# Attention in a hybrid decoder block: every second block of 512 queries computed with the keys on the partitions, the others still with weights transposed by DMA

## The chip, the cores and the metric

The kernel runs on one core of one Trainium2 chip. The metric is the device time of one execution in microseconds (us). An engine is named as the profile names it: PE is the matrix engine (its weight loads are PEld), DVE the vector engine, ACT the scalar engine, POOL the general engine and SP the queue engine, which here only issues DMAs.

## What is computed

One layer of a decoder block on 4096 tokens, with 16 learned meta tokens in front. The normalised input is projected; one half of the columns feeds eight attention heads with a forgetting bias, the other eight heads of a recurrence (RWKV-7). Both halves are gated, projected out, added to the input and normalised. The part that the change touches is the attention:

```python
def _fox_block(q, k, v, cq, ck, q_start):
    qb, kb = q.shape[2], k.shape[2]
    s = jnp.einsum('bhqd,bhkd->bhqk', q, k).astype(jnp.float32) / math.sqrt(HEAD_DIM)
    s = s + cq[..., :, None] - ck[..., None, :]
    q_pos = q_start + jnp.arange(qb)
    k_pos = jnp.arange(kb)
    s = jnp.where(k_pos[None, :] <= q_pos[:, None], s, NEG_INF)
    p = jax.nn.softmax(s, axis=-1)
    return jnp.einsum('bhqk,bhkd->bhqd', p, v.astype(jnp.float32))

def fox_branch(p, b_f):
    q, k, v, fl, z = _split(p, FOX_SIZES)
    ...
    log_f = jax.nn.log_sigmoid(fl.astype(jnp.float32) + b_f.astype(jnp.float32))
    c = jnp.cumsum(log_f, axis=1).transpose(0, 2, 1)
    ...
    return (o * jax.nn.silu(z.astype(jnp.float32))).astype(p.dtype)
```

Head dimension 64, 8 heads, causal. The term cq is the same for all keys of a query, so the softmax does not need it; the term ck stays.

## The kernel before

**Stages.** First comes a stage of about 2100 us in which the recurrence runs as a chain of small matmuls, and the input projections run beside it as filler. The projections are cut into four passes over the 17 blocks of the input `u`: pass 0 is what the recurrence needs, pass 1 is q, k, v and gate of head pair 2 (heads 4 and 5), pass 2 is head pairs 0 and 1, pass 3 is head pair 3 and the gate of the recurrence (`gate_block`). A unit is 48 matmuls of 256 columns. Then comes the attention: heads in the order of `HEADS` (4, 5, 0, 1, 2, 3, 6, 7). What is left of passes 2 and 3, and after it `rwkv_out` (32 rows of output projection of the recurrence, 24 matmuls of 512 columns each), is the filler of the first seven heads. Beside the last head and after it stands the output projection of the attention (`out_prep`, `out_rows`), 32 rows again.

**Attention before.** Queries go by tiles of 128 (32 tiles a head, `advance` and `attention`). For a tile with W keys before it (W = 16 + 128(i+1)): PE multiplies the query tile with the keys in pieces of 1024 (two matmuls of 512 columns for each 512 keys, since q is kept as a high and a low half in float16); DVE adds the forgetting bias `cb`, writes the scores `sp` to SBUF and keeps the maximum in `mt` (line 1051, followed by a read of the accumulator); ACT takes the exponential and sums the row (line 1065); ACT copies the high half to float16 (line 1071), POOL (60 in 100) or DVE (40 in 100) makes the low half (line 1076). Now the weights lie with queries on the partitions, and the product with V needs keys there, so SP issues a DMA transpose for each piece of up to 1024 keys, both halves, `ht<-hl` (line 1078). PE then multiplies `ht` with V, for every 128 keys one matmul of 128 columns (high half, V as high and low) and one of 64 (low half). DVE and ACT finish the 64 output columns (lines 1096 to 1101). In the program the product of tile i is written behind the scores of tile i+1.

**Order.** A scheduler puts the instructions of each engine into a fixed order when the kernel is built; `tc.high_priority` sets what goes first (attention 100000, its filler 97000; for the last head attention has 3000). Each engine runs its list strictly in that order and waits where an operand isn't there. Buffers rotate: 6 of `hl`, 6 of `ht`, 9 of `sp`, 2 PSUM tiles of 1024 scores. Loads for attention (Q, K, V, `cb`) are issued on ACT's queue.

Of the kernel before, what the change touches and what calls it, by code (L numbers as in the profile page):

```python
# [37 lines left out]
NREST = 26  # L38
SEG = 1024
CH = 1024  # L40
NHL, NSP = 6, 9
HEADS = (4, 5, 0, 1, 2, 3, 6, 7)
POOL_SHARE = 60
FILL = 1.0
PASS_OF = (2, 2, 1, 3)
# [5 lines left out]
P_SHIFT = 15 * math.log(2.0)  # L51
# [25 lines left out]
def hymba_kernel(ctx: ExitStack, tc, x, meta, norm_w, w_in, b_f, mu_shift, w0, w_up, a0, a_up,  # L77
# [141 lines left out]
    qk_d = [dram.tile([5, P, TP], F16, name=f"qk_d{p}") for p in range(4)]  # L219
# [12 lines left out]
    scs = const.tile([P, 4, 2, 2], F32, name="scs")  # L232

# [5 lines left out]
    with ExitStack() as rs:  # L239
# [223 lines left out]
        def qk_block(p, w, bi, u):  # L463
# [4 lines left out]
            qk = fi.tile([P, 5, NB], F16, tag="qk", name="qk")  # L468
# [3 lines left out]
            for j in range(2):  # L472
                s = w["sq"] if j == 0 else UNSCALE * QK_SCALE
                A.activation(qk[:, 3 * j, :n], ps[:, j, :n], AF.Copy, scale=s)
                V.scalar_tensor_tensor(out=qk[:, 3 * j + 1, :n], in0=ps[:, j, :n], scalar=s, in1=qk[:, 3 * j, :n],
                                       op0=ALU.mult, op1=ALU.subtract)
            G.tensor_copy(qk[:, 2, :n], qk[:, 0, :n])
            fq.dma_start(qk_d[p][:, :, t0:t0 + n].rearrange("a p t -> p a t"), qk[:, :, :n])

        def vz_block(p, w, bi, u):  # L480
# [11 lines left out]
            A.activation(vt[:m, :ns, :, 0, :], pv, AF.Copy, scale=UNSCALE * QK_SCALE)  # L492
            for s in range(ns):
                V.scalar_tensor_tensor(out=vt[:m, s, :, 1, :], in0=pv[:, s], scalar=UNSCALE * QK_SCALE,
                                       in1=vt[:m, s, :, 0, :], op0=ALU.mult, op1=ALU.subtract)
# [53 lines left out]
        def forget():  # L549
# [23 lines left out]
            for j0 in range(0, NJ, 2):  # L573
# [11 lines left out]
                SP.dma_start(c_d[:, j0 * P:(j0 + k) * P], row[:, :k * P])  # L585
                yield 0.1
# [9 lines left out]
            pair_units(0) + pair_units(1),  # L596
            pair_units(3) + [unit(gate_block, wd[4 + j], j) for j in range(2)]]
# [3 lines left out]
                ((2, 2), (1, 0), qk_weights(1, wd[1], wp1)), ((2, 3), (1, 1), vz_weights(1, wd[1], wp1)),  # L601
                ((3, 0), (2, 0), qk_weights(3, wd[3], wp1)), ((3, 1), (2, 1), vz_weights(3, wd[3], wp1)),
                ((3, 2), (2, 2), gate_weights(0, wd[4], wp1)), ((3, 3), (2, 3), gate_weights(1, wd[5], wp1))]
        ended = (-1, 0)
        done = [0] * 4
# [30 lines left out]
        def projections():  # L636
            for i in range(4):
                yield from run_pass(i)
# [323 lines left out]
    with ExitStack() as fs:  # L962
        def apool(name, bufs, **kw):
# [3 lines left out]
        NCH = SEQ // CH  # L967
        fw = apool("fw", 1)
        kv = apool("kv", NCH + 1)
        ps_q = apool("ps_q", 2, space=PSUM)  # L970
# [4 lines left out]
        V.tensor_copy(identb, ident)  # L975
        dmask = fw.tile([P, P], BF16, name="dmask")
        G.memset(dmask, 0.0)
        G.affine_select(out=dmask, in_=dmask, pattern=[[-1, P]], compare_op=ALU.is_ge, fill=-1e30,
                        base=0, channel_multiplier=1)

        def projected(p, t):

            while done[PASS_OF[p]] * NB < min(t, SEQ + 1):
                next(late)

        def head_load(h, c):
# [6 lines left out]
            Kt = kv.tile([P, CH + N_META], F16, tag="K", name="K")  # L993
            for a in range(2):
                DQ.dma_start(Kt[64 * a:64 * a + 64, :n], qk_d[p][3 + a, q0:q0 + 64, ta:ta + n])
# [4 lines left out]
            Vt = kv.tile([P, CH // P + 1, P], F16, tag="V", name="Vt")  # L1000
            DQ.dma_start(Vt[:, :CH // P], v_d[p][ta:ta + CH, hp * P:hp * P + P].rearrange("(j t) e -> t j e", t=P))
            if n > CH:
                DQ.dma_start(Vt[:N_META, CH // P], v_d[p][SEQ:T, hp * P:hp * P + P])
            return Kt, Vt, cb
# [7 lines left out]
        qz = {}  # L1012

        def attention(h, i, head, dst):

            nonlocal nseg
            p, hp = divmod(h, 2)
            q0 = 64 * hp
            if i % 4 == 0:
                g = min(4, NT - i)  # L1020
                t0 = N_META + i * P
# [264 lines left out]
```

## Time and profile before

| | us |
|---|---|
| three runs | 4457.58, 4472.32, 4473.12 |
| median | 4472.32 |
| the profiled execution | 4462.28 |
| its span (first to last instruction) | 4460.4 |
| mean granted PE clock of it | 0.916 |

Busy time in that span: PE 3912.1 us (88%), DVE 2956.9 (66%), POOL 2230.5 (50%), ACT 2122.7 (48%). The difference of about 2 us between the execution's time and its span lies around the first and the last instruction. The first attention score matmul starts at 2122.0 us, the last value product near 4361 us; what follows is output projection alone. "Busy" is the time in which an engine works on at least one instruction; for PE, whose matmuls overlap, it says less than the pace at which matmuls follow each other.

### The profile page before, as it was taken

How to read it: one execution, taken by the hardware profiler on the slowest of the kernel's cores; microseconds unless marked ns; L12 is line 12 of the kernel's file. 1: busy time of each engine (PE TensorE's matmuls, PEld its weight loads, DVE VectorE, ACT ScalarE, POOL GpSimd, SP SyncE). 2: the span in 40 equal slices, each digit the busy share in tenths (PEclk: the TensorE clock that was granted, in tenths of full speed). 3: DMA queues.
4: the chain of work that ended last, by engine and by line, in shares of the span. 5: the costliest groups of instructions: out<-in, count | busy, mean ns of one | idle time of the engine just before them, and what ended most of it. 6: DMA issues, size and time to landing. Idle time of an engine off the chain costs nothing. (4 is left out here: it accounts for less than half of the span.)

```text
span 4460.4 us, 106426 instructions
## 1 busy us (share of the span) xinstructions
PE 3912.1 (88%) x42336; PEld 3012.8 (68%) x42336; DVE 2956.9 (66%) x6217; ACT 2122.7 (48%) x4338; POOL 2230.5 (50%) x3289
## 2 busy tenths in 40 slices
PE   5689999999989899998878878888888878978888
PEld 4577777777767677777656655666666656666566
DVE  5346665666667666752878978677787758646774
ACT  5433333333333233321666757577676747524552
POOL 4137565667666665762445545444454435332340
PEclk8899999999876899899999989999999989989989
DMA  9963223323222344324999999999999999999995
GB/s 265 262 172 93 79 79 97 87 75 90 74 70 79 85 138 121 98 88 141 196 213 229 216 193 227 199 216 227 208 212 234 212 203 223 258 270 242 198 218 185
DMA packets 1702644, 755.37 MB, mean 169 GB/s; under 512 B 1444601, under 2 KB 1639601, under 8 KB 1692162
## 3 DMA queue, kind: packets, MB, share of 16 engines
q1 hardware_dynamic: 1489346, 502.84, 55.8%
q10 hardware_dynamic: 194624, 170.08, 15.3%
q0 software_dynamic: 18176, 75.66, 5.6%
q8 instruction: 332, 5.44, 0.5%
q14 instruction: 166, 1.36, 0.1%
HBM read 278.97 MB, written 158.50 MB: 98 GB/s over the span
## 5 line engine op out<-in xcount | busy, mean ns | idle before, releaser
L1076 POOL TENSOR_TENSOR hl<-sp,hl 128x1024 f16<-128x1024 f32 (+7 forms) x384 | 719.7, 1881 | 517.3 <-ACT hl L1071 440.7
L1065 ACT ACTIVATE sp<-sp,nm 128x1024 f32<-128x1024 f32 (+8 forms) x672 | 644.5, 962 | 223.5 <-DVE nm L1057 175.6
L1071 ACT ACTIVATE hl<-sp 128x1024 f16<-128x1024 f32 (+8 forms) x672 | 568.2, 872 | 366.1 <-DMA ht<-hl 239.4
L92 PE MATMUL ps_o<-Vt,ht 128*128 128x64 f16 (+3 forms) x8960 | 559.5, 211 | 180.6 <-DMA ht<-hl 177.8
L92 PE MATMUL ps_q<-K,Q 128*128 128x512 f16 (+4 forms) x2432 | 596.9, 366 | 119.4 <-DVE mt L1051 118.3
L758 POOL TENSOR_TENSOR tm<-X,Am 128x248 f32<-128x248 f32 (+30 forms) x1023 | 498.1, 487 | 376.6 <-DMA Am<-a_d 290.1
L92 PEld LDWEIGHTS <-ht 128*128 128x128 f16 (+1 forms) x8960 | 466.9, 100 | 315.0 <-DMA ht<-hl 204.9
L92 PEld LDWEIGHTS <-wu 128*128 128x128 f16 (+1 forms) x5476 | 513.1, 102 | 194.8 <-ACT wu L160 28.1
L760 POOL TENSOR_TENSOR X<-X,tm 128x248 f32<-128x248 f32 (+30 forms) x1023 | 517.7, 506 | 76.6
L67 PEld LDWEIGHTS <-wu 128*128 128x128 f16 (+1 forms) x4988 | 454.5, 101 | 114.3 <-issue 26.0
L1051 DVE CUSTOM_DVE_ANT_0 sp<-ps_q,cb,mt 128x1024 f32<-128x1024 f32 (+8 forms) x416 | 436.1, 1048 | 80.3 <-PE ps_q L92 40.8
L1076 DVE TENSOR_TENSOR hl<-sp,hl 128x1024 f16<-128x1024 f32 (+8 forms) x288 | 383.2, 1333 | 99.3 <-ACT hl L1071 98.1
L92 PEld LDWEIGHTS <-Q 128*128 128x128 f16 x2432 | 221.8, 100 | 294.8 <-issue 150.2
L67 PE MATMUL ps_in<-fu,wu 128*128 128x256 f16 x3108 | 416.0, 285 | 3.4 <-DVE car L67 3.4
L1051 DVE CUSTOM_DVE_ANT_0 sp<-ps_q,cb,scs 128x1024 f32<-128x1024 f32 (+7 forms) x256 | 297.6, 1164 | 71.2 <-POOL hl L1076 43.9
L92 PE MATMUL ps_qk<-fu,wu 128*128 128x256 f16 x1632 | 237.7, 280 | 24.0 <-DVE t1k L500 18.5
L92 PE MATMUL ps_vz<-wu,fu 128*128 128x256 f16 x1644 | 247.6, 284 | 1.0 <-ACT th L544 0.6
L92 PE MATMUL ps_p<-OH,yH 128*128 128x512 f32 x512 | 221.5, 433 | 29.0 <-DVE oxt L1144 27.5
L1070 POOL MEMSET hl<- 128x224 f16 x256 | 72.4, 287 | 336.8 <-DMA ht<-hl 318.4
L92 PE MATMUL ps_zr<-fu,wu 128*128 128x256 f16 x1536 | 224.8, 285 | 8.0 <-DVE nm L1057 6.3
L67 PE MATMUL psz<-UV,SC 32*64 32x64 f32 (+1 forms) x4128 | 222.4, 232 | 3.0 <-ACT UV L67 2.2
L92 PE MATMUL ps_p<-OH,yL 128*128 128x512 f32 x512 | 209.6, 411 | 0.0
(350 smaller groups left out, 6976.6 us busy)
## 6 DMA issues: line engine op xcount, KB each, us to landing
fu<-u_d POOLq DMA_DIRECT2D x32, 1024.0 KB, 6.8
fu<-u_d SPq DMA_DIRECT2D x30, 1024.0 KB
pr<-p_d SPq DMA_DIRECT2D x32, 832.0 KB
p_d<-prt SPq DMA_DIRECT2D x96, 256.0 KB
u_d<-u SPq DMA_DIRECT2D x16, 1024.0 KB
Am<-a_d SPq DMA_DIRECT2D x128, 128.0 KB
Q<-qk_d ACTq DMA_DIRECT2D x128, 128.0 KB
oxt<-in_x_dram ACTq DMA_DIRECT2D x32, 512.0 KB
```

The source lines that it names most:

```text
L67: r = f(*args, **kw)
L92: PE.matmul(o, lhsT=l, rhs=r, start=start, stop=stop)
L758: G.tensor_tensor(out=tm[:, :, :k], in0=bc(X[:, :, s:s + 1], [P, 8, k]), in1=bc(Am[:, s * C + s + 1:s * C + C].unsqueeze(1), [P, 8, k]), o ...
L760: G.tensor_tensor(out=X[:, :, s + 1:], in0=X[:, :, s + 1:], in1=tm[:, :, :k], op=ALU.add)
L1051: V.tensor_tensor_reduce(out=sp[:, a - a0:b - a0], in0=ps[:, :b - a], in1=head[c][2][:, a - o:b - o], scale=scs[:, p, 0, hp:hp + 1], scala ...
L1065: A.activation(sp[:, :n], sp[:, :n], AF.Exp, bias=nm[:, 0:1], accum_out=nm[:, 1 + a // SEG:2 + a // SEG])
L1070: G.memset(hl3[:, :, n:], 0.0)
L1071: A.activation(hl3[:, 0, :n], sp[:, :n], AF.Copy)
L1076: eng.tensor_tensor(out=hl3[:, 1, :n], in0=sp[:, :n], in1=hl3[:, 0, :n], op=ALU.subtract)
```

## The change

The eight blocks of 512 queries of a head go by turns. Blocks 1, 3, 5 and 7 (`straight(n)`) are computed as before, in the new function `weights_s`, with these differences: score pieces are 512 wide instead of 1024 (four PSUM tiles of 512 instead of two of 1024), the row sum is no longer made by ACT's accumulator but by a column of ones beside V (products of 129 and 65 columns), and the output is finished once for a block in `finish`. Blocks 0, 2, 4 and 6 are computed in `weights` with the keys on the partitions: PE makes the transposed scores (128 keys by 512 queries) directly, in two matmuls, of which the second also adds the shift by the maximum, carried in rows 64 to 127 of `QL` against a constant in `KB`; ACT's exponential reads PSUM and adds the key's bias from the new tile `cneg` as its per-partition bias; the result already has keys on the partitions and needs no transpose. For the shift the maximum of each query must be known beforehand: `maxima(n+1)`, run beside block n, makes scores once more from the high half alone (one matmul per 512 keys) and reduces them on DVE.

Buffers: `hl` 5, `ht` 4, `sp` 6. The projections now go in five passes, one head pair each (2, 0, 1, 3), with the two gate units beside pairs 0 and 1, so `u` is read once more. `qk_d` loses its third row, and POOL the copy that filled it. A row of `rwkv_out` counts 1.0 instead of 0.5 in the filler's budget, a straight block gets 1.6 times the filler of another, and what `projected` forces ahead is counted. In the last head, rows of output projection are offered after every second step once a block is finished.

```diff
+CH = 1024
+NHL, NSP, NHT = 5, 6, 4
 SEG = 1024
-NHL, NSP = 6, 9
+LAG = 2
+SHARE_S = 1.6
-PASS_OF = (2, 2, 1, 3)
+PASS_OF = (2, 3, 1, 4)
...
-            pair_units(0) + pair_units(1),
-            pair_units(3) + [unit(gate_block, wd[4 + j], j) for j in range(2)]]
+            pair_units(0) + [unit(gate_block, wd[4], 0)],
+            pair_units(1) + [unit(gate_block, wd[5], 1)],
+            pair_units(3)]
...
+    def maxima(n):
...
+            for t in range(NQ):
...
+                    ps = ps_q.tile([P, 512], F32, tag="q", name="ps_m")
+                    mm(ps[:, :e - a], QA[:, t * P:(t + 1) * P], head[c][0][:, a - o:e - o], True, dg == e)
...
+                    V.tensor_tensor_reduce(out=sx[:, :e - a], in0=ps[:, :e - a], in1=head[c][3][:, a - o:e - o],
+                                           scale=1.0, scalar=(-3e38 if ni == 0 else mt[:, ni - 1:ni]),
...
+            psb = ps_q.tile([P, QB], F32, tag="q", name="ps_b")
+            for t in range(NQ):
+                for v in range(2):
+                    mm(psb[64 + 32 * v:96 + 32 * v, t * P:(t + 1) * P], bc(bp[:, t, v:v + 1], [P, 32]), identh)
+            A.activation(QL[64:128], psb[64:128], AF.Copy)
...
+    def weights(n):
...
+            for j0 in range(0, J, 2):
...
+                    ps = ps_q.tile([P, QB], F32, tag="q", name="ps_s")
+                    mm(ps[:k, qa:], head[c][0][:, o:o + k], QA[:, qa:], True, False)
+                    mm(ps[:k, qa:], head[c][1][:, o:o + k], QL[:, qa:], False, r < 0)
...
+                    A.activation(sp[:k, v, qa:], ps[:k, qa:], AF.Exp, bias=cneg[:k, j, h:h + 1],
+                                 scale=scs[:k, p, 0, hp:hp + 1])
...
+                    A.activation(hh[:k, v, qa:], sp[:k, v, qa:], AF.Copy)
+                    nseg += 1
+                    eng = G if nseg * POOL_SHARE % 100 < POOL_SHARE else V
+                    eng.tensor_tensor(out=hl[:k, v, qa:], in0=sp[:k, v, qa:], in1=hh[:k, v, qa:], op=ALU.subtract)
...
+                            mm(po, hh[:kk, v, ts], Vj[:kk, 0:HD2], j == 0 and t % 2 == 0, False)
+                            mm(po[:, HD:], hl[:kk, v, ts], Vj[:kk, HD:HD2], False, t % 2 == 1 and r == t + 1)
...
+                pend.append(out)
+                while len(pend) > LAG:
+                    pend.pop(0)()
...
+    def straight(n):
+        return blocks_a[n][1] % 2 == 1
...
+            u, k = units(n), 0
+            for i, _ in enumerate((weights_s if straight(n) else weights)(n)):
+                while k * u < steps * (i + 1):
+                    next(nxt, None)
+                    k += 1
+                yield
```

Two places in the built order show what moved. The first is DVE's list in the second head of the order, in the block of queries 2576 to 3087 (block 5). Names: `sp` or `spq` are a tile's own scores, `mt` its running maximum, `sx` the scores that only feed a maximum of the block after it; `ISA` with two outputs is the fused add and maximum, `ISA` with one is the read of its accumulator. Before:

```order
L1051 ISA sp_33638,mt_33623<-ps_q_33639,cb_31742,mt_33623,scs_121 128x1024
L1051 ISA mt_33623 128x1
L1096 TENSOR_REDUCE nm_33495<-nm_33495 128x1
L1097 RECIPROCAL nm_33495<-nm_33495 128x1
L1076 TENSOR_TENSOR hl_33413<-sp_33329,hl_33413 128x1024
L503 SCALAR_TENSOR_TENSOR t1k_33293<-t1k_33294,t1k_33293 128x256
L1100 TENSOR_TENSOR o1_33241<-ps_o_33192,o1_33241 128x64
L1076 TENSOR_TENSOR hl_33419<-sp_33337,hl_33419 128x16
L1051 ISA sp_33645,mt_33623<-ps_q_33646,cb_32516,mt_33623,scs_121 128x272
```

And now, in the same block:

```order
L1203 ISA spq_33860,mt_33817<-ps_q_33881,cb_30230,mt_33817,scs_121 128x512
L1203 ISA mt_33817 128x1
L1084 ISA sx_33887,mt_33831<-ps_m_33885,cb_31835,mt_33831 128x512
L1084 ISA mt_33831 128x1
L1203 ISA spq_33911,mt_33817<-ps_q_33912,cb_31835,mt_33817,scs_121 128x512
L1203 ISA mt_33817 128x1
L1084 ISA sx_33918,mt_33831<-ps_m_33916,cb_31835,mt_33831 128x512
L1084 ISA mt_33831 128x1
L1203 ISA spq_33911,mt_33817<-ps_q_33920,cb_31835,mt_33817,scs_121 128x144
```

The block's own reductions are half as wide, and between them stand those of the next block's maxima, one for one.

The second is ACT's list: exponentials (`sp`), copies to float16 (`hl`, `hx`) and DMA issues. Before, in and behind a tile with 3728 keys:

```order
L1065 ACTIVATE sp_34198,nm_34227<-sp_34198,nm_34227 128x1024
L1065 ACTIVATE sp_34205,nm_34227<-sp_34205,nm_34227 128x1024
L1065 ACTIVATE sp_34212,nm_34227<-sp_34212,nm_34227 128x1024
L1065 ACTIVATE sp_34219,nm_34227<-sp_34219,nm_34227 128x656
L1071 ACTIVATE hl_34086<-sp_33993 128x528
L474 ACTIVATE qk_33766<-ps_qk_33765 128x256
L1071 ACTIVATE hl_34296<-sp_34198 128x1024
```

Now, at the end of a block with the keys on the partitions, where the next block's queries are loaded:

```order
L1139 ACTIVATE sp_33675<-ps_s_33682,cneg_122,scs_121 128x400
L1139 ACTIVATE sp_33730<-ps_s_33732,cneg_122,scs_121 128x272
L1144 ACTIVATE hx_33676<-sp_33675 128x512
L1139 ACTIVATE sp_33730<-ps_s_33739,cneg_122,scs_121 128x144
L1061 DMA QA_33823<-qk_d2_102 64x512
L1139 ACTIVATE sp_33778<-ps_s_33780,cneg_122,scs_121 16x16
L1144 ACTIVATE hx_33676<-sp_33675 128x400
L1061 DMA QA_33823<-qk_d2_102 64x512
```

The exponential reads PSUM in pieces of at most 512, and no transpose stands behind the copy.

## Rows read from the trace of the kernel before

**Rows 1.** Busy time by stretch (stretch, its length, engines, clock, DMA share, GB/s).
```profile
2115.00:4460.00 2345.00, 1978.27 (x18471) 1471.32 (x18469) 1699.27 (x3476) 1415.85 (x2704) 1005.04 (x923) 0.93 1.09 218
2410.00:2583.00 173.00, 147.42 (x1598) 109.57 (x1596) 151.74 (x287) 127.55 (x236) 90.76 (x77) 0.94 1.14 216
2583.00:2660.00 77.00, 56.53 (x554) 40.56 (x555) 56.69 (x144) 39.57 (x87) 35.85 (x45) 0.84 1.10 203
4362.00:4460.00 98.00, 85.43 (x384) 67.32 (x382) 49.23 (x72) 23.87 (x43) 8.11 (x15) 0.97 0.51 186
```

**Rows 2.** SP's queue in the second head's middle, its transposes over the run, their waiters.
```profile
2408.93 180.16 SPq L1078 DMA_TRANSPOSE ht<-hl  x62
...
L1078 SPq DMA_TRANSPOSE ht<-hl x672: 1167/2134/12831, 2125.6 to 4347.2; - x168
...
  POOL hl L1070: 318.4, 99
...
  PE ps_o L92: 177.8, 87
```

**Rows 3.** Matmuls in stretches where PE runs without a gap (chain; timeline for the third).
```profile
4255.05 0.86 PE ps_q L92 x4
4263.96 0.69 PE ps_o L92 x16
...
2046.82 4.53 PE L67 MATMUL ps_vz<-wu,fu 128*128 128x256 f16 x40
...
4381.74 5.71 PE ps_p L92 x24
```

**Rows 4.** PE by line and shape in the stretch 2410 to 2583.
```profile
L92 PE MATMUL ps_q<-K,Q 128*128 128x512 f16 x193 | 52.0, 389 | 12.0 <-DVE mt L1051 11.7
L92 PE MATMUL ps_o<-Vt,ht 128*128 128x128 f16 x392 | 44.5, 223 | 10.8 <-DMA ht<-hl 10.8
L92 PE MATMUL ps_qk<-fu,wu 128*128 128x256 f16 x251 | 34.8, 273 | 0.0
L92 PE MATMUL ps_vz<-wu,fu 128*128 128x256 f16 x214 | 32.9, 291 | 0.0
```

**Rows 5.** DVE by line and shape (the second row from 2250 to 3750 alone).
```profile
L1051 DVE CUSTOM_DVE_ANT_0 sp<-ps_q,cb,mt 128x1024 f32<-128x1024 f32 x216 | 289.1, 1339 | 41.1 <-PE ps_q L92 27.8 <-POOL hl L1076 4.6 <-DVE mt L1051 3.0
...
L1051 DVE CUSTOM_DVE_ANT_0 sp<-ps_q,cb,mt 128x656 f32<-128x656 f32 x18 | 17.1, 952 | 1.0 <-PE ps_q L92 0.8 <-DVE mt L1051 0.2
...
L1051 DVE CUSTOM_DVE_ANT_0 sp<-ps_q,cb,scs 128x1024 f32<-128x1024 f32 x200 | 255.3, 1276 | 56.9 <-POOL hl L1076 33.3 <-PE ps_q L92 20.8 <-PE ps_o L92 0.7
L1051 DVE DVE_READ_ACCUMULATOR2_ANT mt<- 128x1 f32 x672 | 54.5, 81 | 0.0
L1076 DVE TENSOR_TENSOR hl<-sp,hl 128x1024 f16<-128x1024 f32 x176 | 271.5, 1543 | 53.3 <-ACT hl L1071 52.4 <-DMA Zt<-zf_d 0.6
L1101 DVE SCALAR_TENSOR_TENSOR yo<-o,nm,Zt 128x64 f32<-128x64 f32 x256 | 158.2, 628 | 1.6
```

**Rows 6.** ACT by line and shape (the second row from 2250 to 3750), and a load's issue.
```profile
L1065 ACT ACTIVATE sp<-sp,nm 128x1024 f32<-128x1024 f32 x416 | 473.6, 1140 | 172.0 <-DVE nm L1057 144.5 <-DVE ss L181 4.3 <-DMA out_dram<-oxt 4.2
...
L1065 ACT ACTIVATE sp<-sp,nm 128x656 f32<-128x656 f32 x24 | 20.0, 832 | 4.0 <-POOL hl L1070 2.7 <-DVE nm L1057 1.3
...
L1071 ACT ACTIVATE hl<-sp 128x1024 f16<-128x1024 f32 x416 | 430.0, 1050 | 193.9 <-DMA ht<-hl 126.1 <-issue 17.5 <-PE ps_q L92 9.8
L1065 ACT ACTIVATION_READ_ACCUMULATOR sp<-sp,nm 128x1 f32 x672 | 127.4, 190 | 0.0
...
L1025 ACTq DMA_DIRECT2D Q<-qk_d x128: 581/620/5495, 2106.0 to 4203.4; - x128
```

**Rows 7.** The first score matmul, and the stores of the last head (first and last start).
```profile
L92 PE MATMUL ps_q<-K,Q x2432: 169/379/635, 2122.0 to 4319.0; 128*128 128x512 f16 x145, 128*128 128x16 f16 x13, 128*128 128x272 f16 x11, 128*128 128x144 f16 x10
...
L1185 ACTq DMA_DIRECT2D yf_d<-yo x32: 326/388/1485, 4032.0 to 4362.7; - x32
```

**Rows 8.** A piece of the chain that ended last: how long a transpose took.
```profile
4238.93 8.57 DMA ht<-hl
```

## What the change was predicted to do

> **What bounds the kernel now.** I read the busy time by stretch first. From 2115 us to the end the attention and the late projections run, 2345 us in all, with PE busy 1978 us of it, DVE 1699, ACT 1416, POOL 1005 [rows 1]. No engine is full over the whole stage. In the middle of a head (2410 to 2583) PE is busy 85%, DVE 88%, ACT 74%; where one head ends and the next begins (2583 to 2660) PE falls to 73% and its granted clock from 0.94 to 0.84 [rows 1]. The last 98 us are output projection alone.
>
> Then SP's queue: in the middle of that head 62 transposes stand in 180 us with no other work in the list, 2.9 us each, and over the run 672 of them with a median of 2.1 us [rows 2]. POOL waited 318 us and PE's products 178 us for a transpose's landing [rows 2]. So the transposes and DVE hold the middle of a head together, and PE follows closely.
>
> For PE I need the pace, not the busy time. Where it runs without a gap, a 512-column score matmul takes 0.215 us (0.86/4), two value products of 128 and 64 columns together 0.086 us (0.69/8), a projection matmul of 256 columns about 0.109 us (4.53 less its own run-out, over 40), an output matmul 0.238 us (5.71/24) [rows 3]. With the counts of the middle of that head (193, 392, 251 and 214 matmuls [rows 4]) PE's work at pace is 193 x 0.215 + 392 x 0.086 + 465 x 0.109 = 126 us, and some 7 us of small pieces, so 133 of 173 us, 0.77 of the time. Over the whole stage: 4224 tiles of 128 by 128 scores x 2 x 0.054 = 454 us, 4480 pairs of products x 0.086 = 386, 4950 projection matmuls x 0.109 = 540, 1536 output matmuls x 0.238 = 366, masks 18; together 1764 of 2345, 0.75.
>
> **The change part by part.**
>
> Transposes. Of 8960 transposed tiles 4992 stay (blocks 1, 3, 5, 7), 56%. SP's queue, occupied some 672 x 2.1 to 2.9 us = 1430 to 1950 us now, is needed for 800 to 1090 us. It stops being what holds a whole head, but it stays in half of the blocks.
>
> PE. Added: 1856 tiles of maxima x 0.054 = 100 us; 160 more masks and 256 small matmuls that spread the shift, about 23 us; 174 more projection matmuls that the new order puts behind the first score, 19 us, which the stage before it loses. Two extra columns in the value products are 3 us. The sum is 145 us more, 1909 us at pace. A head's attention goes from 107 to 123 us.
>
> Where the filler lies. The order puts 1236, 1278, 1208 and 1234 projection matmuls into the first four heads (606, 720, 613 and 836 before), 168 into the fifth and none later; the 32 rows of recurrence output go into heads six and seven (456 and 312 matmuls). So a head of the first four has 123 + 1239 x 0.109 = 258 us of PE work at pace, the fifth 141, the next two 231 and 197.
>
> DVE. A reduction costs 1.05 us per 1000 columns ((1339 - 952)/368) and 0.26 us besides, plus 0.08 us for the accumulator's read [rows 5]; halving its width doubles the fixed part: 1216 instructions instead of 672, 544 x 0.34 = 187 us more, less 0.06 us where the scale is a constant in place of a column (1339 against 1276 [rows 5]), 33 us. Gone: the line that finishes a tile, 256 x 0.63 = 158 us [rows 5], and some 60 us of small ones. DVE's total falls by about 60 us, but it isn't spread any more: a head's straight blocks carry their own reductions (84, 61 us), the reads (12 us), the next blocks' maxima (68, 45 us), subtractions (20 pieces of at most 1.54 us, 23 us) and 5 us of small ones, 146 us; blocks with the keys on the partitions leave DVE nearly idle.
>
> ACT. The row sums go (672 x 0.19 = 127 us [rows 6]); exponentials in pieces of 512 pay the fixed 0.28 us twice. In the other half of a head: 68 exponentials, 44 us; copies, 34 us; small ones 5 us; DMA issues, about 40 of 0.6 us each [rows 6], 25 us. Together 108 us, against PE's 123 us for both halves. ACT bounds that half wherever there is little filler.
>
> Small edits, one answer each: the fifth pass reads `u` once more, 16 loads hidden behind a DMA share that falls; the transposes of `cneg` are 33 tiny matmuls; POOL loses a copy. Each at nothing; if their cover failed, some 10 us.
>
> The end. Before, 14 rows of output projection stand behind the last value product: 98 us [rows 1], 7 us a row. Now 5 do: 35 us and some 8 for the longer last block, 43. The other 9 rows move into the last head, which has 123 + 648 x 0.238 = 277 us of PE work at pace and took 330 us (4032 to 4362 [rows 7]); I leave it at 335.
>
> The sum. Start of attention 2122 [rows 7] less 19: 2103. First four heads: the work at pace over a share of the time. The bounds are 0.77 (middle of a head now) and 0.98 (2047 to 2051, projections alone); I take 0.90, nearer the upper one, because filler is at hand throughout and SP and DVE need 0.5 to 0.65 of the time there: 258/0.90 = 287, four times 1147. Fifth head: straight half DVE 146 to 150, other half ACT 108, 258. Heads six and seven the same with a little more for evictions, 262 each, 524. Last head 335, end 43. Together 2103 + 1147 + 258 + 524 + 335 + 43 = 4410, with the 2 us around it 4412 against 4462 of the profiled execution, 50 us less. The median of the three runs is 10 us above that execution, so I predict 4420.
>
> **The rivals.**
>
> First, the transposes were all that held the kernel. Then the first four heads run at 0.95 (272 each), the halves of the later heads overlap down to their larger engine total (about 225 each) and the last head drops to 310: 2103 + 1088 + 675 + 310 + 43 + 12 = 4231. For it speaks the waiting for landings [rows 2]; against it that DVE was busier than PE in the middle of a head.
>
> Second, a wait takes the place of the one removed: 0.85 in the first four heads (304 each) gives 4410 + 68 + 12 = 4490, inside what no change means.
>
> Third, slower: the halves don't overlap, and each of the 28 turns from a straight block to one without transposes in the first seven heads ends with transposes in flight. One takes 8.6 us near the end of the chain [rows 8]; the value products behind it hold up the PSUM tiles of the next block. At 10 us a turn, with half covered by filler, 140 us: 4560. It decides from 2 us of uncovered wait a turn on, since 28 x 1.8 us is the forecast's whole gain. For it speaks the loss at the head's end now [rows 1], against it that the built order lets the next block's scores pass before those products.
>
> Fourth, the transposes aren't a holder at all. In the middle of a head the queue has 62 of them back to back in 180 us [rows 2]; should those durations be only waiting of its own, then freeing it gives nothing and the stage keeps its 0.75: 1909/0.753 = 2535, and 2103 + 2535 + 12 = 4650. [...]
>
> **How the numbers follow.** Chances: forecast (4340 to 4450) 0.40, first rival 0.15, second 0.17, third 0.20, fourth 0.08. Half a per cent of 4472, 22 us, is about what a measurement of this kernel can tell from no change, so faster means under 4450: 0.40 + 0.15 = 0.55; same 0.17; slower 0.20 + 0.08 = 0.28. Cases of both signs hold much of the chance; the forecast's own range is 4340 to 4450. The range for 8 in 10 reaches from 4250 to 4580: it leaves out the lower third of the first rival (0.05), the fourth (0.08) and the upper end of the third (0.06).
>
> **What would show it.** In the changed profile: 384 transposes, SP's queue with gaps as long as half a head; PE busy 95% or more in the first four heads and their length near 287 us; DVE over 85% busy in straight blocks and under 40% in the others; the fifth head near 258 us; 5 rows of output projection behind the last value product, 43 us. If the first four heads take over 305 us with PE waiting for `ht`, the third rival is right; if PE stands at 0.75 at pace with SP idle, the fourth. The forecast is wrong above all if ACT in the blocks without transposes, or DVE in the straight ones, is held by something that the rows of before can't show, such as a PSUM tile that comes free late.

## The result, and the profile after

The changed kernel takes 4812.32 us (median of 4 runs, 4796.29 to 4834.09) against 4472.72 us before; the ratio is 1.0759, 95% interval 1.0697 to 1.0820. It is slower by 340 us, where 4420 was predicted and 4580 was the upper end. The profiled execution took 4814.22 us, its span is 4812.5 us.

Busy time by stretch answers to [rows 1] (columns as there). The first stretch is the whole of attention. The next two lie in the fifth head, which has hardly any filler: the straight block 7, and the last 20 us of block 6 before it, from the end of block 5 on (its own scores had begun at 3605). The last is what stands behind the last head.

```profile
2115.00:4766.00 2651.00, 2168.45 (x19321) 1538.49 (x19318) 1638.98 (x3857) 1431.73 (x2162) 1157.37 (x1356) 0.90 0.71 147
3650.00:3738.00 88.00, 46.66 (x396) 28.57 (x394) 52.16 (x126) 42.20 (x54) 31.56 (x38) 0.71 0.94 154
3630.00:3650.00 20.00, 16.92 (x174) 10.04 (x175) 11.51 (x31) 12.52 (x23) 14.51 (x22) 1.00 0.14 38
4766.00:4812.00 46.00, 32.43 (x136) 25.94 (x136) 16.60 (x24) 7.83 (x14) 2.70 (x5) 0.83 0.34 117
```

Attention starts where it was expected, at 2105, and ends with 46 us of output projection. In between it is long, and no engine is full. In the straight block PE is busy 53% at a granted clock of 0.71 (0.50 from 3690 to 3700 and from 3710 to 3720, 1.00 from 3730 to 3738), DVE 59%, and the DMA engines 0.94. In the stretch of the block with the keys on the partitions PE is busy 85% at a granted clock of 1.00 and the DMA engines 0.14. In these stretches each kind holds one resource and leaves the other idle.

The transposes and who waits for them answer to [rows 2] (the second number of the three is the median, in ns; the waits are us and times):

```profile
L1227 SPq DMA_TRANSPOSE ht<-hl x352: 1167/2506/26202, 2129.7 to 4760.5; - x176
...
  PEld L97: 381.7, 158
  PE ps_o L97: 325.5, 134
  POOL hl L1219: 225.8, 40
```

There are 352 of them in place of 672, and PE's products waited 325 us for their landing where it was 178. SP itself waited mostly for something to transpose; the blocks that have no transposes are among these waits (what it waited for, us in all, times, the longest):

```profile
SPq L1227 <- DVE hl L1225: 620.7, 54, 140.0
SPq L1227 <- POOL hl L1225: 566.8, 67, 47.5
```

Measured against the terms of the sum, with the heads' ends read from the last product on POOL that writes `yo`:

| stretch | forecast | changed kernel | without the transposes (d_no_tr, below) |
|---|---|---|---|
| start of attention | 2103 | 2105 | 2107 |
| first four heads | 1147 | 1362 | 1193 |
| fifth head | 258 | 271 | 247 |
| heads six and seven | 524 | 661 | 587 |
| last head | 335 | 367 | 326 |
| end | 43 | 47 | 48 |

A piece of the chain of waits in that straight block answers to [rows 8] (start, length, what): one landing of 18 us, one of 4 before it, and two of 10 together behind it.

```profile
3672.30 4.25 DMA ht<-hl
...
3681.23 18.38 DMA ht<-hl
...
3721.32 10.13 DMA ht<-hl x2
```

Most of the loss lies in the heads with filler. In the fifth head, which has hardly any, the forecast was nearly met.

### The profile page after: what moved, and what is told of

It is laid out like the page before. It is cut to its first block, busy times and chain, and to the rows that moved or that the text cites. A ratio compares the mean times of both kernels' runs of the same rounds, so it can differ in the third digit from the quotient of the medians.

```text
span 4812.5 us, 108451 instructions
## 1 busy us (share of the span) xinstructions
PE 4133.0 (86%) x43329; PEld 3104.6 (65%) x43329; DVE 2904.9 (60%) x6607; ACT 2155.6 (45%) x3843; POOL 2360.4 (49%) x3706
## 4 chain that ended last, share of the span: by engine, by line
PE 24%; DMA 17%; issue 6%; ACT 4%; DVE 4%; POOL 3%; ACTq 1%; SPq 1%; POOLq 0%; DVEq 0%
DMA ht<-hl 13%; PE ps_o L97 5%; PE ps_p L97 4%; PE ps_s L97 2%; PE ps_q L97 2%; PE ps_vz L97 2%; PE ps_qk L97 2%; POOL hl L1225 2%; PE ps_zr L97 2%; ACT sp L1139 1%; DVE spq L1203 1%; DMA cb<-c_d 1%; PE ps_m L97 1%; ACT spq L1214 1%; DMA QA<-qk_d 1%
## 5 line engine op out<-in xcount | busy, mean ns | idle before, releaser
L97 PE MATMUL ps_o<-Vt,ht 128*128 128x65 f16 (+3 forms) x4992 | 373.8, 223 | 326.2 <-DMA ht<-hl 325.5
L97 PEld LDWEIGHTS <-wu 128*128 128x128 f16 (+1 forms) x5248 | 490.6, 101 | 166.1 <-ACT wu L165 25.4
L72 PEld LDWEIGHTS <-wu 128*128 128x128 f16 x5216 | 475.0, 101 | 129.2 <-issue 27.4
L1225 POOL TENSOR_TENSOR hl<-spq,hl 128x1024 f16<-128x1024 f32 (+3 forms) x193 | 408.6, 2129 | 305.2 <-ACT hl L1220 291.4
L1214 ACT ACTIVATE spq<-spq,nm 128x1024 f32<-128x1024 f32 (+4 forms) x352 | 334.5, 1008 | 430.7 <-DVE nm L1210 253.6
L1203 DVE CUSTOM_DVE_ANT_0 spq<-ps_q,cb,mt 128x512 f32<-128x512 f32 (+4 forms) x544 | 396.5, 730 | 73.0 <-PE ps_q L97 46.2
L1139 ACT ACTIVATE sp<-ps_s,cneg,scs 128x512 f32<-128x512 f32 (+4 forms) x544 | 363.8, 734 | 104.0 <-PE ps_s L97 44.0
L1147 POOL TENSOR_TENSOR hx<-sp,hx 128x1024 f16<-128x1024 f32 (+5 forms) x210 | 328.8, 1577 | 151.5 <-ACT hx L1144 137.4
L1220 ACT ACTIVATE hl<-spq 128x1024 f16<-128x1024 f32 (+4 forms) x352 | 305.7, 914 | 71.3 <-DMA ht<-hl 39.4
L97 PE MATMUL ps_o<-Vt,hx 128*128 128x129 f16 (+3 forms) x3968 | 283.7, 210 | 13.7 <-POOL hx L1147 7.6
```

The costliest lines, as they stand in the source:

```text
L72: r = f(*args, **kw)
L97: PE.matmul(o, lhsT=l, rhs=r, start=start, stop=stop)
L1139: A.activation(sp[:k, v, qa:], ps[:k, qa:], AF.Exp, bias=cneg[:k, j, h:h + 1], scale=scs[:k, p, 0, hp:hp + 1])
L1147: eng.tensor_tensor(out=hl[:k, v, qa:], in0=sp[:k, v, qa:], in1=hh[:k, v, qa:], op=ALU.subtract)
L1203: V.tensor_tensor_reduce(out=sp[:, a - a0:e - a0], in0=ps[:, :e - a], in1=head[c][3][:, a - o:e - o], scale=scs[:, p, 0, hp:hp + 1], scala ...
L1214: A.activation(sp[:, :nn], sp[:, :nn], AF.Exp, bias=nm)
```

## Experiments

Times are compared by their ratio to runs of the kernel before on the same chip in the same set (its medians were 4476 to 4490 us); 0.01 is 45 us.

### Which part of the change loses the time

Four kernels: the old kernel with the new buffer counts; the new one with every block of one kind or of the other; the new one without its transposes.

```diff
 a_before_bufs (kernel before)
-NHL, NSP = 6, 9
+NHL, NSP, NHT = 5, 6, 4
-    ht = at.tile(..., name="ht", bufs=NHL)
+    ht = at.tile(..., name="ht", bufs=NHT)
 b_all_straight / c_all_keys (changed kernel)
-            return blocks_a[n][1] % 2 == 1
+            return True        # c_all_keys: False
 d_no_tr (changed kernel, NHL = 9)
-                    SP.dma_start_transpose(out=ht, in_=hl)
-                    hts.append(ht)
+                    hts.append(hl3)
```

> The kernel before with the buffer counts of the changed one and nothing else: 5 hl in place of 6, 6 sp in place of 9, 4 ht in place of 6. A tile of the last block of a head has 4 or 5 pieces of 1024 keys, so 9 sp hold two tiles and 6 hold hardly more than one. Theory 1 (too few buffers: stages that overlapped now run one after the other): 150 to 300 us slower than before, SP's transposes in groups with gaps of several us between the tiles, as in the straight blocks of the changed kernel. Theory 2 (the turns between the two kinds of block lose the time): within 20 us of before. Theory 3 (the transposes never held anything, the stage keeps its pace whatever is done): within 20 us of before.

Measured: 4588 us, 1.0232 (1.0174 to 1.0290), 104 us slower. In the old kernel the buffers cost less than expected, about a third of the loss.

> The changed kernel with every block straight (queries on the partitions, transposed weights), so no turns between kinds, no maxima and 705 transposes again; buffers 5, 6, 4, pieces of 512, five passes and the new tail stay. Theory 1 (too few buffers): no faster than the changed kernel, 4800 to 5000 us, since twice as many blocks now starve. Theory 2 (turns): the 28 turns are gone, so near before, 4450 to 4520. Theory 3: 4450 to 4550, the pace of the stage before.

Measured: 4764 us, 1.0646 (1.0589 to 1.0703). It has 672 transposes, not 705. Taking the alternation away gives back only 0.011. The blocks of one kind lose nearly as much, which no theory had by itself: buffers are 0.023 of it by the run above, 0.04 had no name yet.

> The changed kernel with the keys on the partitions in every block: no transposes of weights at all, maxima for every block (4224 tiles of maxima, about 2040 us of TensorE work at pace in place of 1909). Theory 1 (too few buffers in the straight blocks) and theory 2 (turns): no straight block is left, so about 2103 + 2040/0.90 + 45, 4415 us, faster than both kernels. Theory 3 (a pace of 0.75 to 0.77 whatever is done): 2103 + 2040/0.76 + 45, 4830 us.

Measured: 4571 us, 1.0212 (1.0168 to 1.0256): faster than the changed kernel by 0.055, not than the kernel before, and 156 us above the 4415 of theories 1 and 2. From 2115 to 4330 PE is busy 2079 of 2215 us at a clock of 0.97, so here PE is the bound. Its 2040 us of work in 2408 us of attention are a pace of 0.85, and theory 3 with its 0.76 falls:

```profile
2115.00:4330.00 2215.00, 2079.11 (x19068) 1434.70 (x19066) 1435.85 (x3619) 1468.93 (x2382) 1066.96 (x1450) 0.97 0.31 93
```

> The changed kernel without the transposes of the straight blocks: the value products read the untransposed weights as they stand in hl, of which there are 9 buffers (5 and the 4 of ht). Left out is the transposition, all engines' work is the same. Theory 1 (too few buffers, stages one after the other): without the transposes' 8 us or so in each tile's cycle the straight blocks shorten by about a quarter but sp still has only 6 buffers, 4600 to 4700 us. Theory 2 (turns that end with transposes in flight): all of the loss goes, 4350 to 4450. Theory 3: unchanged, 4780 to 4840.

Measured: 4517 us, 1.0071 (1.0033 to 1.0108). 295 us of the loss go with the transposes, more than theory 1 or a fixed pace allowed and less than theory 2 did. So most of what loses the time lies in the straight blocks and has to do with transposes; 97 us over the forecast of 4420 stay without them. PE's longest waits, the first three of the changed kernel and then of this one:

```profile
PE ps_o L97 <- DMA ht<-hl: 325.5, 134, 35.5
PE ps_q L97 <- DVE mt L1203: 43.9, 41, 6.4
PE psb L97 <- POOL sc L189: 30.6, 9, 11.4
...
PE ps_q L97 <- DVE mt L1203: 33.4, 55, 3.2
PE psb L97 <- POOL sc L189: 31.1, 9, 12.0
PE ps_o L97 <- DVE hl L1225: 30.1, 24, 4.0
```

The wait for the landing went, and less took its place: the value products still waited 115 us in all, for weights that DVE, POOL and ACT were making (339 us in the changed kernel, landings included). The attention of both kernels, from the first score matmul to the last head's end (the changed kernel first):

```profile
2105.00:4766.00 2661.00, 2178.45 (x19416) 1546.70 (x19413) 1643.49 (x3876) 1435.08 (x2170) 1159.40 (x1359) 0.90 0.71 147
...
2107.00:4459.50 2352.50, 2112.85 (x19414) 1513.29 (x19411) 1650.16 (x3876) 1422.51 (x2170) 1167.20 (x1358) 0.95 0.32 97
```

Of the 309 us between them, 243 are idle time of PE; the other 66 are the same work of PE taking longer, at a granted clock of 0.90 in place of 0.95.

### Buffers and the wait for the landing

```diff
 e_566: NHL, NSP, NHT = 5, 6, 6      e_584: NHL, NSP, NHT = 5, 8, 4
 h_tr_unread (d_no_tr with NHL = 7)
+                    SP.dma_start_transpose(out=ht, in_=hl)   # nobody reads ht
                     hts.append(hl3)
 b2_straight_bufs (b_all_straight)
-NHL, NSP, NHT = 5, 6, 4
+NHL, NSP, NHT = 6, 9, 6
-            KB = kv.tile(...)
```

> The changed kernel with 6 ht buffers in place of 4 (5 hl, 6 sp as they are). In a head's last block a tile has 4 or 5 transposed pieces, so with 4 ht the transposes of a tile can't begin before the value products of the tile before it have been read. Theory 1a (ht is the buffer that starves the straight blocks): TensorE's waits for ht fall from 325 us to under 220 and the time by 80 to 150 us, to 4660 to 4730. Theory 1b (sp is): within 30 us of the changed kernel. Theory 2 (landing time itself, not buffers): within 30 us of the changed kernel.

Measured: 4813 us, 1.0745 (1.0685 to 1.0805): no change, PE's wait for `ht` 322 us.

> The changed kernel with 8 sp buffers in place of 6 (5 hl, 4 ht as they are), so that two tiles of 4 pieces fit. Theory 1a (ht starves): within 30 us of the changed kernel. Theory 1b (sp starves: the scores of the next tile wait for the weights of this one): 80 to 150 us faster, 4660 to 4730. Theory 2 (landing time): within 30 us of the changed kernel.

Measured: 4709 us, 1.0518 (1.0466 to 1.0571), 103 us faster. So `sp` is the buffer that was short. PE's products waited 231 us in place of 325 for the landing:

```profile
PE ps_o L97 <- DMA ht<-hl: 230.6, 108, 8.7
```

> As d_no_tr (4517: value products read the untransposed weights in hl), but the transposes into ht are issued all the same and nobody reads ht; 7 hl, 6 sp, 4 ht. So the queue, its traffic and the hold on hl are there, only TensorE's wait for the landing is gone. Left out is the use of the transposed weights. If TensorE's waiting in order for the landing is the price, 4510 to 4570; if the queue's traffic or the late release of hl is, 4700 to 4800.

Measured: 4665 us, 1.0428 (1.0375 to 1.0482), between the two ranges. Half of the 295 us is PE waiting for the landing; the other half stays though nobody reads what is transposed. That half is the traffic, or `hl` coming free later (7 buffers here, 9 in d_no_tr); this run doesn't tell those two apart.

> All blocks straight in the changed frame, as in b_all_straight (4764), with the buffers of the kernel before, 6 hl, 9 sp, 6 ht; the K copy with the shift rows, which only the other kind of block reads, is dropped to make room, and o1 has 2 buffers in place of 4. If the buffers cost in this frame what they cost in the old one (107 us), 4650 to 4670, and the frame alone (pieces of 512, five passes, filler early) costs 180 us. If the buffers are all of it, 4450 to 4520.

Measured: 4641 us, 1.0358 (1.0297 to 1.0419). At equal buffers and with the same 672 transposes, the new frame was 160 us slower than the kernel before. Its SP queue is full (occupied 2099 of 2416 us), but each transposition is dearer:

```profile
L1225 SPq DMA_TRANSPOSE ht<-hl x672: 1167/2863/13533, 2122.9 to 4538.1; - x168
```

2863 ns against 2134 in [rows 2]. Taken packet by packet, a full one (1024 keys, 2048 packets of 256 bytes and 32 small ones) lasted from its first packet to its last 2.64 us at the lower quartile, in the kernel before 2.07, though the median packet took 18 ns in both. In the full ones beside which no other queue moved a packet, the median was 2.55 us against 1.97 in the kernel before, and 12 packets in 100 took over 30 ns against 0.4, so it was not the traffic beside them.

### The address of the buffer that is read

In the built programs `hl` and `ht` begin at multiples of 256 bytes in the kernel before, 96 and 224 bytes behind one in the changed kernel, 128 behind one in b2_straight_bufs. New tiles had moved them. An unused tile of a few bytes moves them back, or off:

```diff
 i_after_aligned (changed kernel)
+   at.tile([P, 32], F32, tag="pad1", ...)      # ahead of ht
+   at.tile([P, 56], F32, tag="pad2", ...)      # ahead of yo
 j_before_off (kernel before)
+   at.tile([P, 8], F32, tag="pad", ...)        # behind ht: hl and ht 32 bytes lower
 n_hl_off: that pad ahead of ht (hl moves)      n_ht_off: and [P, 56] ahead of ht (ht alone moves)
```

> The changed kernel with two unused tiles of 128 and 224 bytes per partition, which move the starts of hl and ht to multiples of 256 bytes in the built program, as they are in the kernel before; in the changed kernel they lie 96 and 224 bytes behind one. Nothing else differs. In the trace a full transposition (1024 keys) takes from its first packet to its last 2.64 us at the lower quartile, in the kernel before 2.05 with the same packets. Theory A (the address makes transposes dearer): the quartile falls to 2.05 to 2.1 and, with 352 pieces by 0.6 us of which most lies on TensorE's waits, 4600 to 4720 in place of 4812. Theory B (other traffic makes them dearer): within 25 us of the changed kernel.

> The kernel before with one unused tile of 32 bytes per partition, which moves hl and ht to 224 bytes behind a multiple of 256; nothing else differs. Theory A (address): full transpositions from 2.05 to about 2.6 us at the lower quartile; the queue is nearly full there, 672 pieces by 0.45 us and more, 120 to 280 us slower, 4600 to 4760. Theory B (other traffic): within 25 us of before.

> The kernel before with one unused tile of 32 bytes that moves hl (and what lies ahead of it, sp among them) to 224 bytes behind a multiple of 256, ht stays on one. With both moved it took 4671. If the address that is read by the transposition makes it dearer, 4640 to 4700 and a lower quartile of 2.6 us; if the one that is written does, 4455 to 4500 and 2.05.

> The kernel before with two unused tiles that move ht alone to 224 bytes behind a multiple of 256, hl stays on one. If the address that is written makes the transposition dearer, 4640 to 4700 and a lower quartile of 2.6 us; if the one that is read does, 4455 to 4500 and 2.05.

| kernel | hl, bytes behind 256 | ht | full transposition, lower quartile | ratio to before |
|---|---|---|---|---|
| before | 0 | 0 | 2.07 us | 1 |
| j_before_off | 224 | 224 | 2.61 | 1.0425 (1.0361 to 1.0488) |
| n_hl_off | 224 | 0 | 2.60 | 1.0358 (1.0284 to 1.0433) |
| n_ht_off | 0 | 224 | 2.03 | 0.9990 (0.9943 to 1.0037) |
| changed | 96 | 224 | 2.64 | 1.0759 |
| i_after_aligned | 0 | 0 | 2.04 | 1.0571 (1.0499 to 1.0643) |

The rows of the transposes, in the order j, n_hl, n_ht, i (one from each trace):

```profile
L1078 SPq DMA_TRANSPOSE ht<-hl x672: 1167/2633/15268, 2133.3 to 4539.2; - x168
...
L1079 SPq DMA_TRANSPOSE ht<-hl x672: 1167/2546/19870, 2138.7 to 4522.0; - x168
...
L1079 SPq DMA_TRANSPOSE ht<-hl x672: 1167/2108/15958, 2128.4 to 4354.0; - x168
...
L1228 SPq DMA_TRANSPOSE ht<-hl x352: 1167/1906/14158, 2138.6 to 4645.9; - x176
```

Theory A held each time, though i_after_aligned (4730 us) came out 10 us above its range. 32 bytes make the kernel before 190 us slower, and in these runs it is the address that the transposition reads that counts (2.60 us at the lower quartile in n_hl_off), not the one it writes (2.03 in n_ht_off). In the changed kernel the address costs 0.019, 84 us, with intervals that put it between about 0.01 and 0.03.

```diff
 k_straight_aligned: b2_straight_bufs with hl, ht at multiples of 256
 l_aligned_584: i_after_aligned with NHL, NSP, NHT = 5, 8, 4
```

> b2_straight_bufs (all blocks straight, the buffers of before, 4641) with hl and ht at multiples of 256 bytes in place of 128 behind one; an unused mask is dropped to make room. Theory A (address): the rest of the frame costs little, 4470 to 4530. Theory B (other traffic, or pieces of 512 and the five passes): 4610 to 4670.

Measured: 4460 us, 0.9964 (0.9924 to 1.0003), no slower than before. Pieces of 512, the five passes and what else the frame changed together cost nothing that can be told; all that b2_straight_bufs lost was the address (0.039).

> The changed kernel with hl and ht at multiples of 256 bytes and 8 sp in place of 6. Theory A (address) and too few sp together: 4709 less 100 to 150, 4550 to 4620. Theory B: 4680 to 4730. If it stays above the 4517 of the kernel without transposes by more than 50 us, the landing of a tile's transposes inside the straight blocks has a price of its own that neither buffers nor addresses take away.

Measured: 4656 us, 1.0411 (1.0358 to 1.0464): between the ranges of the two theories. Address and `sp` give back 0.035 of 0.076. It stays 0.034, 139 us, above d_no_tr, so the price of its own that the expectation names is there.

### The alternation itself

```diff
 r_straight_584: k_straight_aligned with NHL, NSP, NHT = 5, 8, 4
 m_by_head (changed kernel, aligned, NHL, NSP, NHT = 6, 8, 4; KB for heads 5 to 7 alone)
-            return blocks_a[n][1] % 2 == 1
+            return n // NBQ not in (4, 5, 6)
 m_by_head_584: NHL = 5           s_two_heads: (4, 6) in place of (4, 5, 6)
```

> k_straight_aligned (all blocks straight, hl and ht at multiples of 256 bytes, 4460) with 5 hl, 8 sp, 4 ht, the buffers of l_aligned_584 (4656). Theory A (what is left of the loss is the alternation: in the straight blocks nothing lies beside the waits for a tile's transposes): under 4540. Theory B (what is left is the missing hl and ht buffers): 4610 to 4670, no better than the kernel that alternates.

> Both kinds of block, but by head: heads 1 to 4 and the last straight, heads 5 to 7 with the keys on the partitions; hl and ht at multiples of 256 bytes, 6 hl, 8 sp, 4 ht. The first four straight heads of k_straight_aligned end at 3123 us, the three heads of c_all_keys take 220, 338 and 250, the last straight head 260 and its end 94: 4285, with dearer straight heads by the fewer buffers (up to 20 each) and the change of kind twice 4300 to 4400. Theory A (the kinds lose when they change every block): in that range, faster than both kernels. Theory B (blocks of 512 with few buffers lose by themselves): 4450 to 4550.

> m_by_head (4460) with 5 hl in place of 6, so with the buffers 5, 8, 4 of l_aligned_584, where the kinds change by block (4656), and of r_straight_584, where all blocks are straight (4533). Theory A (the alternation by block is what is left of the loss): 4470 to 4560, at least 100 below the kernel that alternates by block. Theory B (the blocks with the keys on the partitions or the buffers are): 4600 to 4660.

> m_by_head with only heads 5 and 7 on the keys' side, head 6 straight. In m_by_head heads 5, 6 and 7 took 280, 370 and 277 us with the filler of heads 5 and 6 on a full TensorE (0.99 of the clock); in k_straight_aligned head 6 took 310. If straight heads carry filler better than the others, 4400 to 4450; if a change of kind costs more than that, 4460 to 4490.

| blocks, hl and ht at multiples of 256 | hl, sp, ht | time | ratio to before |
|---|---|---|---|
| l: kinds change by block | 5, 8, 4 | 4656 | 1.0411 (1.0358 to 1.0464) |
| r: all straight | 5, 8, 4 | 4533 | 1.0096 (1.0052 to 1.0141) |
| m_584: kinds change by head | 5, 8, 4 | 4478 | 1.0006 (0.9957 to 1.0055) |
| m: kinds change by head | 6, 8, 4 | 4460 | 0.9931 (0.9893 to 0.9969) |
| s: two heads by keys | 6, 8, 4 | 4470 | 0.9985 (0.9938 to 1.0032) |

Theory A held in r and m_584: at equal `hl`, `sp` and `ht` and equal addresses, changing the kind at every block costs 0.031 against one kind, and 0.040 against the two kinds by head (three heads of eight by keys, in place of half of the blocks). m_by_head came out at 4460, in theory B's range, where theory A had 4300 to 4400. Its fifth and sixth heads had 1232 and 1231 matmuls of filler, where c_all_keys had none in the fifth, and took 280 and 370 us for the 220 and 338 of the estimate; its first four took 1068 for 1009. It is still the only version here that beats both kernels by more than its interval, by 0.007. s_two_heads fell into the second of its ranges; fewer heads by keys gain nothing that can be told, since its interval overlaps that of m_by_head.

In b_all_straight, taking the alternation away had seemed to give back only 0.011; that kernel has nearly twice as many of the dearer transposes, and its `sp` was short too.

Two stretches of l (two rows), then of m_584 (two rows), the second stretch being m_584's heads by keys:

```profile
2400.00:3150.00 750.00, 657.52 (x6685) 495.83 (x6684) 490.75 (x1200) 445.64 (x706) 367.44 (x455) 0.93 0.73 150
3150.00:4000.00 850.00, 688.38 (x6044) 475.23 (x6042) 526.89 (x1282) 456.14 (x671) 386.58 (x446) 0.89 0.75 158
...
2400.00:3150.00 750.00, 626.43 (x6469) 463.54 (x6468) 558.53 (x1343) 470.67 (x659) 403.26 (x427) 0.93 1.11 212
3150.00:4000.00 850.00, 809.80 (x7202) 576.35 (x7201) 550.35 (x1325) 507.24 (x824) 395.46 (x543) 0.99 0.45 130
```

By head, one resource is taken up in each stretch: the DMA engines in straight heads (share 1.11; above 1, since the times of packets in flight together are added up: in the kernel before 17.5 packets were in flight on average from 2115 to 4460, 1.09 for each of 16 engines), PE in heads by keys (95% busy, clock 0.99). By block neither is. Where the straight blocks lose shows in SP's queue. In blocks 1, 3, 5 and 7, from the last transposition of a tile to the first of the next tile, the queue stood idle 466 us in l (96 such gaps, 4.9 us each) and 82 us in r (0.86 each); all transposes of these blocks took 1495 us from first to last in l, 1301 in r. So most of it isn't the turn itself: inside a straight block that alternates, the next tile's weights are not ready when the queue has sent this tile's. In between stand what the all-straight kernel doesn't have there: the maxima of the next block, on PE and DVE, and more filler (in each of the first four heads 794 to 938 of its matmuls, counted from one block's end to the next, in these four blocks; in r 441 to 515).

## Why the prediction was wrong, step by step

**The step that failed** is the pace of the first four heads: "I take 0.90, nearer the upper one, because filler is at hand throughout and SP and DVE need 0.5 to 0.65 of the time there". The share was right: SP was occupied 1065 us, within the 800 to 1090 of the forecast. But a share says nothing of when. All of it falls into half of the blocks, and there PE, in order, stood before products whose `ht` had not landed, with the filler behind them: 325 us over the run in 134 waits, of which the longest, 35.5 us, ended at 3088.9, and the next filler, 25 matmuls, began at 3091.1. The upper bound of 0.98 held nothing either: the 0.109 us that it is worked out with come from the same stretch. PE was to be busy 95% or more there and was 85%. The first four heads ran at 1032 / 1362 = 0.76, as the kernel before. Without the transposes they ran at 1032 / 1193 = 0.86, so 169 of the 215 us there go with them. Heads six and seven lost 137 us, of which 74 go with them. What stays without a transposition, 46 and 63 us, shows that 0.90, and the 262 us for each of heads six and seven, were too good even for a kernel with no landing to wait for.

**Three things make up the loss against the kernel before**, and the forecast had a price for none (the first two together gave back 0.035 of 0.076, the third is as large as the rest):
- `NHL, NSP, NHT = 5, 6, 4`. The prediction has no word on these buffer counts, although the diff shows them. A tile of block 7 has 4 or 5 pieces; 6 `sp` don't hold two tiles. 103 us for `sp` alone in the changed kernel, 104 for all three counts in the old one.
- The duration of a transposition was taken from [rows 2] as if it were a property of the operation. It belongs to the buffer's address too: 84 us here. No row of before could show it; the addresses in the two built programs could.
- The change of kind at every block: 0.031 to 0.040, 140 to 180 us; it shows between the tiles of the straight blocks, where SP's queue stood idle 466 us in l and 82 in r.

**The third rival** had the right sign and half the right idea, in the wrong place. By the prediction's own test (heads over 305 us with PE waiting for `ht`) it is the one that came. But it put 10 us on each of 28 turns, at the end of a straight block. Of the 325 us that PE waited for a landing, sorted by the tile whose product waited, 49, 139, 79 and 59 us fall on the four tiles of a block: only the last 59 are at a turn. The rest is inside the block, from its first tile on, and 181 us of it in block 7. Its bound of 4560 was therefore too low.

**The fourth rival** gave nearly the right pace (0.75; 1909 / 2661 = 0.72 came out), for a reason that is refuted: with the transposes taken away the time falls by 295 us, so they do hold it. **The first rival**'s premise, that they alone did, falls with d_no_tr: without one transposition its first four heads run at 0.86, not at 0.95.

**DVE** was to be over 85% busy in straight blocks and under 40% in the others; it is 59% and 58% in the two stretches of the fifth head shown above. It waits in the straight one, and in the other 8 of its 11.5 us already reduce the scores of the next block. The count of 384 transposes was wrong too: 5, 9, 13 and 17 pieces make 44 a head, 352.

**What was right:** start of attention (2103, measured 2105), the end (43; 47), the fifth head (258; 271) and, less nearly, the last head (335; 367, of which 41 go without the transposes). The 108 us for half a head by keys came out in c_all_keys, whose fifth head has no filler and takes 220 us for both halves; that ACT is what bounds it was argued and isn't shown, since ACT (fourth of the busy times) is busy 79% there and PE 85% at a clock of 0.91:

```profile
3372.00:3592.00 220.00, 186.69 (x1725) 104.84 (x1724) 158.46 (x413) 173.32 (x273) 117.18 (x163) 0.91 0.15 40
```

**What stays open:** what of h_tr_unread's half is traffic and what is `hl`; what holds d_no_tr 97 us above the forecast; and whether the 4.9 us between two tiles of a straight block are the next block's maxima or the filler between its scores, which were not tried apart.

## What to carry to other kernels

A resource that is needed half of the time on average can still be the whole bound of half of the blocks (here SP's queue was occupied 1065 of 2661 us, and the DMA share was 0.94 in the stretch of a straight block and 0.14 in that of the other kind): price a change of kind at the wait inside one block, and let two kinds with different bounds alternate over long stretches, as by head here (0.040 better than by block), unless they really run at the same time. Read buffer counts in a diff as edits with a price, pieces of a tile against buffers. And when tiles are added to a pool, look at where the others have moved: compare the duration of the same transfer in two traces before explaining it by load.

## What the runs showed of the hardware

In these runs a transposition of 1024 keys with two halves, from one SBUF buffer to another, took 2.07 us at the lower quartile in the kernel before and 2.04 in i_after_aligned, where the buffer that it reads begins at a multiple of 256 bytes. It took about a quarter more where that buffer begins behind one: 2.64 us at 96 bytes (the changed kernel), 2.60 and 2.61 at 224 (n_hl_off, j_before_off). At 128 bytes (b2_straight_bufs) the median over pieces of all sizes was 2863 ns, at a multiple in the same frame (k_straight_aligned) 2224. 224 bytes on the side that is written made no difference (2.03 us, n_ht_off). 2048 of the 2080 packets of such a transposition have 256 bytes. Of 16 engines' time its queue took 39.6% in the changed kernel and 34.9% with the address put right, for the same bytes in the same window (packets, MB, share; the changed kernel first, i_after_aligned second):

```profile
q1 hardware_dynamic: 650240, 163.62, 39.6%
...
q1 hardware_dynamic: 650240, 163.62, 34.9%
```

The transposition of 1024 keys took 1.29 times as long 96 bytes behind a multiple (2.64 to 2.04 us) and 1.26 times as long 224 bytes behind (2.61 to 2.07). The median packet took 18 ns in the kernel before and in the changed one alike; in the changed kernel's full transposes beside which no other queue moved a packet, 12 packets in 100 took over 30 ns. What makes those packets longer no run shows.

One transposition took ten times the median of 2506 ns beside loads: the 26202 ns in the row of the changed kernel began at 3061 us, behind `K`, `cb` and `fu` loads issued from 3048 to 3054, and a product of PE waited 35 us for it (start, length, instruction, and in brackets the idle time before it):

```profile
3048.53 1.10 ACTq L1017 DMA_DIRECT2D K<-qk_d  x2
3051.31 0.34 ACTq L1021 DMA_DIRECT2D cb<-c_d  x1
...
3049.33 0.55 POOL L405 DMA_DIRECT2D fu<-u_d  x1
...
3088.91 1.27 PE L97 MATMUL ps_o<-Vt,ht 128*128 128x129 f16 x13 [35.45 <-DMA ht<-hl]
```

In the kernel before the longest transposition was 12.8 us [rows 2]. That the loads caused it is read from their place in time, not tried.
